# Two places for the squares of q, and modulation products called two loads later

## The chip, the cores and the metric

The kernel runs on one core of one Trainium2 chip. A core has a matrix engine (TensorE, "PE" in the profile), a vector engine (VectorE, "DVE"), an activation engine (ScalarE, "ACT"), a general engine (GpSimd, "POOL") and a synchronisation engine (SyncE, "SP"), which here issues most of the DMA transfers. Each engine works through its own instructions in order and waits on semaphores for the others. The metric is the time of one execution on the device in microseconds. Three runs of the kernel before took 1590.62, 1590.85 and 1592.18 us; the median is 1590.85.

## The reference, cut to what matters

The model is one layer of a diffusion transformer over 1024 latent tokens and 256 context tokens with 1024 channels, all in float32. What the stage of this case computes is:

```python
mod = jax.nn.silu(c) @ w_mod[l] + b_mod[l]                    # six vectors of 1024
mod_c = jax.nn.silu(c_ctx) @ w_mod[l, :, :2 * D_MODEL] + ...  # two vectors of 1024
h = x * (1.0 + scale1) + shift1
h_c = ctx * (1.0 + mods_c[1]) + mods_c[0]
proj = h @ w_in + b_in       # q, k, v of branches A and B, and 2 x 1024 gate logits
q_b = rope(rms_norm(q_b) * q_norm_g)
```

Behind it come windowed attention (branch A) and global attention (branch B), a gated merge, an output projection, a LayerNorm, a SwiGLU feed-forward part with a convolution, and a second LayerNorm. The q norm of branch B needs the mean square of each of the 8 heads of 64 columns for each token.

## The kernel before

Float32 accuracy is had from three passes: each operand is split into a high half (a cast to the fp32r format) and a low half (the rest), and `mm3` (lines 88 to 90) multiplies high by high, low by high and high by low. A split is a cast (line 80 on ACT, 82 on POOL or 84 on VectorE) and a subtraction (line 85) on VectorE or POOL. The names start with "wh" and "wl" for the two halves of a weight.

The projection stage runs in passes. The first makes h from x and projects q of branch B (q1acc). Then a fixed list, `order`, follows: three gate tiles, the pass qa (q of branch A, tokens 0 to 511), four gate tiles, qb (q of branch A, the other tokens), four gate tiles, ka (keys and values of five token tiles), one gate tile, kb, four gate tiles. A gate tile is 2 halves of 24 matmuls; a pass has 8 steps k, each with 3 matmuls for each of its token tiles: 4 in qa and qb, 5 in ka and kb. In each step `prefetch` loads and splits weights some steps ahead, the matmuls follow, then `mods` and `side_step` are called.

Weights are loaded into three "raw" tiles and split into eight "wp" tiles (four pairs of high and low half), so a load waits for the split of an earlier weight, and a cast waits until TensorE is done with an earlier pair. Gate weights have their low half made on POOL, the others on VectorE.

*The ring.* `ht` takes the oldest of 19 free tile places of 128 x 1024 values (`hfree`), and `hput` gives a place back to the end of the list. A tile that is made for a short time is taken and given back at once (`tmp`), so its place comes round again when all free places ahead of it have been used. A load into a place waits until the last use of the tile that had it before. In this stage the ring holds the rope tables, the rows silu(c) and silu(c_ctx) (`sc`, `scc`), the q tiles, the tile of squares `sqq`, and short-lived ones: the modulation rows `wml` (line 648) and the gates `sg` (line 666), which are written to memory (`sgd`).

*Modulation.* Of the 64 products of a column of w_mod with silu(c) or silu(c_ctx), 48 are made in this stage, spread evenly over the matmuls up to the end of ka: `mods` loads a row of 512 KB (line 648) and calls `mod`, one VectorE instruction of 128 x 1024 with a sum (line 186), which shows as CUSTOM_DVE and a short read of the accumulator. The first 16 make `modx`, with which the context tiles `cx` are modulated on ACT (line 631); the others make `modc`.

*The squares.* For each of the 8 token tiles of q of branch B, `qpost` has a step s1: ACT squares the tile into one half of `sqq` (line 280), VectorE sums it by heads (line 283) and scales (284), POOL takes the power -1/2 (285) and makes the negative (320). The step s2 turns q by the rope tables (lines 261 to 269), on VectorE or, for every third tile, on POOL. `sqq` has two halves, used in turn, so the square of tile t overwrites what the reduce of tile t-2 reads.

*The order of instructions.* Nobody writes the order out in this stage. A planner (the tile framework) takes the instructions in the order of the calls as their priority, plays the program through with its own costs, and gives each engine at each moment the first instruction that is ready by its reckoning. The order that comes out is fixed, and on the chip each engine keeps to it, also where an instruction that was ready in the plan has to wait in fact. Only from the first LayerNorm on is the order of TensorE written by hand.

Of the kernel before, what the change touches and what calls it, by code (L numbers as in the profile page):

```python
# [13 lines left out]
P = 128  # L14
# [42 lines left out]
UE = "vector", "vector", "vector", "vector", "vector", "gpsimd", "gpsimd"  # L57
LN2_P = 2, 2, 2
GAP = 1
LN1_S = slice(0, 512), slice(512, 768), slice(768, 1024)  # L60
VOFF = 0.0
VSPAN = 1.0
# [5 lines left out]
def layer_kernel(  # L68
# [25 lines left out]
    def ctile(shape, dt, name):  # L94
        return const.tile(shape, dt, tag=name, name=name)
# [4 lines left out]
    bmc = ctile([P, 48], F32, "bmc")  # L100
# [10 lines left out]
    pqs, nqs = (cvt[:, n * 64:n * 64 + 64].rearrange("p (a b) -> p a b", b=8) for n in (0, 1))  # L111
# [19 lines left out]
    def ht(name, shape=(P, T), dt=F32):  # L131
        hslot[name] = pool, tag = hfree.pop(0)
        return pool.tile(list(shape), dt, tag=tag, name=name, bufs=1)

    def hput(*names):
        for n in names:
            hfree.append(hslot.pop(n))
# [27 lines left out]
    def bias_tile(src, nm):  # L165
        b = ph1.tile([P, 512], F32, tag="bias", name=nm, bufs=2)
        nc.sync.dma_start(b, src.partition_broadcast(P))
        return b
# [11 lines left out]
    def tmp(name):  # L180
        t = ht(name)
        hput(name)
        return t

    def mod(w, row, bias, o):
        nc.vector.tensor_tensor_reduce(out=w, in0=w, in1=row, scale=1.0, scalar=bias, op0=ALU.mult, op1=ALU.add,  # L186
                                       accum_out=o)
# [17 lines left out]
    def modulate(k):  # L205
        wm, x, wr = st1.pop(k)
        w = wsplit(wr, f"qb{k}")
        for j in (0, 1):
            col = j * 8 + k
            mod(wm[j], sc, bmc[:, col:col + 1], modc[:, col:col + 1])  # L210
        hh = hTp.tile([P, T], R32, tag="hT", name=f"hh{k}", bufs=16)
        hl = hTp.tile([P, T], R32, tag="hT", name=f"hl{k}", bufs=16)
        a, b = modc[:, k:k + 1], modc[:, 8 + k:9 + k]
        for s in [slice(0, HALF), slice(HALF, T)] if k == 0 else [slice(0, T)]:
            nc.scalar.activation(hh[:, s], x[:, s], AF.Identity, bias=a, scale=b)
            nc.scalar.activation(x[:, s], x[:, s], AF.Identity, bias=a, scale=b)
            nc.vector.tensor_tensor(out=hl[:, s], in0=x[:, s], in1=hh[:, s].bitcast(F32), op=ALU.subtract)
        hT.append((hh, hl))
        return w
# [7 lines left out]
    w = modulate(0)  # L227
    for k in range(KT):
# [8 lines left out]
        w = wn  # L237
# [20 lines left out]
    def rope(eng, dst, src, H, cs, sn, nm, t1=None, t2=None):  # L258
        if t1 is None:
            t1, t2 = pw(f"rt1{nm}"), pw(f"rt2{nm}")  # L260
        eng.tensor_tensor(out=t1.rearrange("p (h d) -> p h d", d=HD), in0=src.rearrange("p (h d) -> p h d", d=HD),
                          in1=bc(cs, H), op=ALU.mult)
        sv = src.rearrange("p (h r a f) -> p h r a f", r=2, a=2, f=16)
        tv = t2.rearrange("p (h r a f) -> p h r a f", r=2, a=2, f=16)
        sg = sn.rearrange("p (r a f) -> p r a f", r=2, a=2)
        for a in (0, 1):
            eng.tensor_tensor(out=tv[:, :, :, a, :], in0=sv[:, :, :, 1 - a, :],
                              in1=sg[:, :, a, :].unsqueeze(1).to_broadcast([P, H, 2, 16]), op=ALU.mult)
        eng.tensor_tensor(out=dst, in0=t1, in1=t2, op=ALU.add)

    def gfold(dst, gi, t, eng):
        eng.tensor_tensor(out=dst[:, 0], in0=ropec[:, t], in1=gcol[:, gi], op=ALU.mult)
        sv = ropes[:, t].rearrange("p (r a f) -> p r a f", r=2, a=2)
        gv = gcol[:, gi].rearrange("p (r a f) -> p r a f", r=2, a=2)
        dv = dst[:, 1].rearrange("p (r a f) -> p r a f", r=2, a=2)
        for a in (0, 1):
            eng.tensor_tensor(out=dv[:, :, a, :], in0=sv[:, :, a, :], in1=gv[:, :, 1 - a, :], op=ALU.mult)

    def rms_scale(x3, H, nm, sq, ss=None):
        nc.scalar.activation(sq.rearrange("p (h d) -> p h d", d=HD), x3, AF.Square)  # L280
        if ss is None:
            ss = ph1.tile([P, 8], F32, tag="ss", name=f"ss{nm}", bufs=4)[:, 0:H]
        nc.vector.tensor_reduce(out=ss, in_=sq.rearrange("p (h d) -> p h d", d=HD), axis=AX.X, op=ALU.add)
        nc.vector.tensor_scalar(out=ss, in0=ss, scalar1=1.0 / HD, scalar2=QK_EPS, op0=ALU.mult, op1=ALU.add)
        nc.gpsimd.tensor_tensor(out=ss, in0=ss, in1=mhalf[:, 0:H], op=ALU.pow)
        return ss
# [14 lines left out]
    def qtile(br, t):  # L301
        return Q[br, t - t % 2][:, t % 2]

    def qpost(br, t):
        q = qtile(br, t)
        q3 = q.rearrange("p (h d) -> p h d", d=HD)
        if br == 0:
            def r0():
                rope(nc.gpsimd if t % 3 == 2 else nc.vector, q, q, 8, ropec[:, t], ropes[:, t], f"q0_{t}")
            return [r0]  # L310
        st = {}

        def s1():
            st["tb"] = ph1.tile([P, 2, HD], F32, tag="tb", name=f"tbq{t}", bufs=4)
            gfold(st["tb"], 0, t, nc.gpsimd)
            rms_scale(q3, 8, f"q{t}", sqq[0][:, t % 2], pqs[:, t])
            if t == NT - 1:
                sqq.clear()
                hput("sqq")
            nc.gpsimd.tensor_scalar(out=nqs[:, t], in0=pqs[:, t], scalar1=-1.0, scalar2=0.0, op0=ALU.mult, op1=ALU.add)  # L320

        def s2():
            tb = st["tb"]
            rope(nc.gpsimd if t % 3 == 2 else nc.vector, q, q, 8, tb[:, 0], tb[:, 1], f"q1_{t}")
        return [s1] + [lambda: None] * GAP + [s2]

    sqq = [ht("sqq", (P, 2, 512))]
    bias_qb = bias_tile(b_qb, "bias_qb")
    for t in range(NT):
        q_evac(1, t, acc[t], bias_qb)  # L330
# [3 lines left out]
    def kv_alloc():  # L334
        KL.extend(ht(f"KL{h}", dt=R32) for h in range(4))
        KC.append(ht("KC", (P, 4, NC), R32))
        VT.extend(ht(f"VT{t}", (P, 2, 4, P), R32) for t in range(5))
# [3 lines left out]
    def kv_post(t, kv):  # L341
# [28 lines left out]
        def s3():  # L370
# [7 lines left out]
            else:  # L378
                nc.scalar.copy(KC[0][:, :, (t - NT) * P:(t - NT + 1) * P], tr)
        return [s1] + [lambda: None] * GAP + [s2, s3]  # L380

# [254 lines left out]
    late = [(col, scc, modx[:, col:col + 1]) for col in range(16)]  # L636
    late += [(col, sc, modc[:, col:col + 1]) for col in range(16, 48)]

    total = len(late)
    span = [0.0, 0.0]  # L640

    def mods(us):
        span[0] += us
        n = total - len(late)
        for _ in range(min(int(total * span[0] / span[1] + 0.01) - n, len(late))):
            col, row, o = late.pop(0)
            w = tmp(f"wml{len(late)}")
            nc.sync.dma_start(w, wmodT[col])
            mod(w, row, bmc[:, col:col + 1], o)
            if not late:  # L650
                hput("sc", "scc")
                kv_alloc()
# [46 lines left out]
    for n, (gi, k) in enumerate(order):  # L699
# [3 lines left out]
        if gi == "g":  # L703
            for hf in (0, 1):
                last = gate(k, hf)
                mods(3 * KT)
                side_step()
            continue
# [4 lines left out]
        w, c = ready.pop((gi, k))  # L713
# [228 lines left out]
    for f in range(2, KT):  # L942
        bT[1, f] = ht(f"bT1_{f}")
        nc.sync.dma_start(bT[1, f], sgd[KT + f])
        w = wb[f // 2]
# [62 lines left out]
    def drain(keep=0):  # L1008
        while len(pend) > keep:
            pend.pop(0)[1]()  # L1010
            clock[0] = 0.0
# [149 lines left out]
    def y_pair(f, s, first=False):  # L1161
        w = s.stop - s.start
        ps = big(f"y{f}_{s.start}_{w}")
        for a in (0, 1):
            mm_ticked(ps[:, a * HALF:a * HALF + w], wts[f + a], mrg, s)
        for a in (0, 1):
            wout_z(f + a, s, ps[:, a * HALF:a * HALF + w], first and a == 0)

    def ln1(si):
        return ln_steps(zs, zq, LN1_S[si], f"a{si}", emit1, LN1_F[si], *LN1_D[si], order=(0, 4, 1, 5, 2, 6, 3, 7))  # L1170

# [11 lines left out]
    for f in (4, 6):  # L1183
        for si in (1, 2):
            y_pair(f, LN1_S[si])
            if f == 6:
# [68 lines left out]
    def up_start(j, gv):  # L1255
        if (j, gv) not in ups:
            if (j, gv) not in upw:
                up_weights(j, gv)
            ups[j, gv] = big(f"u{gv}_{j}"), upw.pop((j, gv)), set()
        return ups[j, gv]  # L1260
# [37 lines left out]
    for j, gv in ((0, 0), (0, 1), (1, 0)):  # L1298
        up_start(j, gv)
    for si, s in enumerate(LN1_S):  # L1300
        drain((len(LN1_S) - 1 - si) * (KT + 3))
        for j, gv in ((0, 0), (0, 1), (1, 0)):
# [235 lines left out]
    w = s.stop - s.start  # L1538
    nt = w // P

    def pst(n, name):
        return ps4.tile([P, HALF], F32, tag=f"r{n}", name=name)
# [55 lines left out]
    for f, done_ in enumerate(((7,), (0,), (1,), (2, 3))):  # L1598
        o = pst(yb[2 + f % 2], f"yl{f}_{r.start}")[:, 0:w]
# [15 lines left out]
    for t, a in OTO:  # L1615
        o = ot[t, a] = ht(f"ot{t}_{a}", (P, HALF))
        nc.vector.scalar_tensor_tensor(out=o, in0=lnr[0][:, a], scalar=mv[:, t:t + 1], in1=zt[a][t], op0=ALU.mult,
                                       op1=ALU.add)
    for t, a in OTO:
        o = ot[t, a]  # L1620
# [125 lines left out]
```

## Time and profile before

| | |
|---|---|
| median of three runs | 1590.85 us |
| the profiled execution | 1593.3 us |
| its span, first to last instruction | 1591.5 us |
| TensorE busy | 97% of the span |
| VectorE, ACT, POOL busy | 74%, 51%, 46% |
| mean granted TensorE clock | 0.993 |
| projections of this case (first gate to the last step of ka) | about 59 to 261 us |

In the rows of the profile L186 is line 186 of the kernel. An instruction is named by its output and inputs, with tile numbers left out (`wml<-wml,sc,bmc`); "x3" is a number of instructions in a group. In the timeline the columns are the start in us from the begin of the span, the duration, the engine, the line, the operation, the tiles and shapes; brackets hold the idle time of the engine before the instruction and what ended it. In a row of waits there stand the waiting engine and line, whom it waited for, and the sum in us, the number and the longest. In a row of the table by stretches there stand the stretch, its length, then for TensorE, its weight loads, VectorE, ACT and POOL the busy time and the number of instructions, then the granted clock, the DMA share and GB/s. In the view of one tile a row gives the smallest, the median and the largest duration in ns and the first and the last start. "SPq" is the queue in which SP issues DMA transfers.

### The profile page before, as it was taken

To read this page: it belongs to the slowest core of one execution; us is meant where nothing else is said; L and a number is where in the kernel's file an instruction comes from. 1 tells how busy PE (TensorE), PEld (TensorE's weight loads), DVE (VectorE), ACT (ScalarE), POOL (GpSimd) and SP (SyncE) were. 2 spreads that over 40 slices of the span, in tenths; PEclk is the share of its full clock that TensorE was granted. 3 is DMA by queue.
4 is the path that set the end of the run, shared out by engine and by line. 5 is a ranking of instruction groups with operands and counts; after the bars stand their busy time and mean duration, and the time that the engine had idled before them with its cause. 6 is when DMAs were issued, how large, how long until landed. Compare 5 with 4: busy or idle time off the path is not lost.

```text
span 1591.5 us, 22189 instructions
## 1 busy us (share of the span) xinstructions
PE 1537.1 (97%) x7748; PEld 1278.4 (80%) x7748; DVE 1181.3 (74%) x1768; ACT 813.3 (51%) x1450; POOL 730.1 (46%) x727
## 2 busy tenths in 40 slices
PE   6999999999999999999999999999999999999997
PEld 5878788878886887777688888888888888888887
DVE  7797646628888777888674778788888788657884
ACT  5422122448888667688521564454444444535552
POOL 0573212426666556665422453566667665021021
PEclk9999999999999999999999999999999999999999
DMA  9685663322227555532451222333334446996731
GB/s 379 218 309 177 214 204 101 118 79 74 64 81 178 136 127 127 125 84 41 141 173 65 80 80 93 106 106 106 106 106 108 117 116 175 368 274 202 260 107 54
DMA packets 112368, 230.00 MB, mean 145 GB/s; under 512 B 12960, under 2 KB 27808, under 8 KB 112160
## 3 DMA queue, kind: packets, MB, share of 16 engines
q1 hardware_dynamic: 96816, 198.93, 37.9%
q0 software_dynamic: 10400, 20.19, 8.3%
q10 hardware_dynamic: 5040, 9.46, 1.6%
q8 instruction: 61, 1.00, 0.3%
q14 instruction: 51, 0.42, 0.1%
HBM read 177.35 MB, written 65.86 MB: 153 GB/s over the span
## 4 chain that ended last, share of the span: by engine, by line
PE 76%; DVE 8%; DMA 7%; ACT 4%; issue 3%; POOL 2%; SPq 0%; DVEq 0%; ACTq 0%; POOLq 0%
PE ptr L529 4%; PE p L89 3%; PE p L88 3%; PE p L90 3%; PE b L90 3%; PE b L89 3%; PE b L88 3%; PE g L88 2%; PE g L89 2%; PE g L90 2%; PE d L89 2%; PE c L89 2%; PE a L89 2%; PE c L90 2%; PE a L90 2%
## 5 line engine op out<-in xcount | busy, mean ns | idle before, releaser
L539 DVE TENSOR_TENSOR ptl<-ptr,pth 128x512 fp32r<-128x512 f32 x188 | 124.7, 685 | 28.2 <-ACT pth L538 25.8
L529 PE MATMUL ptr<-ident,p 128*128 128x128 f32 x816 | 126.6, 278 | 9.5 <-DVE ptl L539 6.9
L538 ACT CAST pth<-ptr 128x512 fp32r<-128x512 f32 x188 | 106.6, 588 | 56.3 <-PE ptr L529 32.6
L85 DVE TENSOR_TENSOR ld<-rd,hd 128x1024 fp32r<-128x1024 f32 x77 | 94.8, 1249 | 50.8 <-ACT hd L80 48.7
L424 ACT ACTIVATE p<-p,nm 128x1024 f32<-128x1024 f32 (+2 forms) x128 | 125.3, 981 | 11.2 <-DVE p L457 10.5
L529 PEld LDWEIGHTS ptr<-ident,p 128*128 128x128 f32 x816 | 93.7, 140 | 39.8 <-DVE ptl L539 13.5
L80 ACT CAST hd<-rd 128x1024 fp32r<-128x1024 f32 x77 | 79.4, 1049 | 81.9 <-PE p L90 55.5
L550 PE MATMUL av<-pth,VT 128*128 128x512 f32 x236 | 104.6, 443 | 1.0 <-ACT avs L556 0.5
L88 PE MATMUL p<-hd 128*128 128x512 f32 x264 | 103.2, 391 | 0.0
L89 PE MATMUL p<-ld,hd 128*128 128x512 f32 x264 | 102.8, 390 | 0.2 <-DVE ld L85 0.2
L90 PE MATMUL p<-hd,ld 128*128 128x512 f32 x264 | 102.7, 389 | 0.0
L88 PE MATMUL g<-hh,whg 128*128 128x512 f32 x256 | 99.9, 390 | 0.0
L90 PE MATMUL g<-hh,wlg 128*128 128x512 f32 x256 | 99.7, 389 | 0.0
L89 PE MATMUL g<-hl,whg 128*128 128x512 f32 x256 | 99.6, 389 | 0.0
L551 PE MATMUL av<-ptl,VT 128*128 128x512 f32 x236 | 97.6, 414 | 2.0 <-POOL ptl L85 1.9
L85 POOL TENSOR_TENSOR wlg<-wg,whg 128x512 fp32r<-128x512 f32 x32 | 45.5, 1428 | 113.3 <-ACT whg L80 83.1
L457 DVE TENSOR_SCALAR_CACHE_REDUCE p<-s,cvt,nmc 128x1024 f32<-128x1024 f32 x64 | 84.5, 1340 | 12.3 <-PE s L413 11.8
L412 PE MATMUL s<-KL,q 128*128 128x512 f32 (+2 forms) x192 | 76.0, 396 | 2.9 <-ACT p_x L424 2.0
L186 DVE CUSTOM_DVE_ANT_0 wml<-wml,sc,bmc 128x1024 f32<-128x1024 f32 x32 | 44.6, 1406 | 43.0 <-DMA wml<-in_wmodT_dram 40.0
L413 PE MATMUL s<-KL,q 128*128 128x512 f32 (+2 forms) x192 | 71.7, 373 | 0.0
L82 POOL TENSOR_SCALAR pth<-prw 128x512 fp32r<-128x512 f32 x48 | 31.1, 648 | 87.6 <-ACT prw L535 62.1
L80 ACT CAST wS<-s 128x512 fp32r<-128x512 f32 x76 | 45.5, 621 | 45.6 <-POOL s L1077 42.8
(420 smaller groups left out, 4959.4 us busy)
## 6 DMA issues: line engine op xcount, KB each, us to landing
wml<-in_wmodT_dram SPq DMA_DIRECT2D x48, 512.0 KB
ru<-in_w_up_dram SPq DMA_DIRECT2D x38, 512.0 KB
rd<-td SPq DMA_DIRECT2D x55, 256.0 KB
rd<-sd SPq DMA_DIRECT2D x44, 256.0 KB
rd<-in_w_dn_dram SPq DMA_DIRECT2D x33, 256.0 KB
wm<-in_wmodT_dram SPq DMA_DIRECT2D x16, 512.0 KB
wg<-in_w_g_dram SPq DMA_DIRECT2D x32, 256.0 KB
sgd<-sg ACTq DMA_DIRECT2D x32, 256.0 KB
```

Of the source, the lines that this page charges most:

```text
L80: nc.scalar.copy(hi, src)
L85: lo_eng.tensor_tensor(out=lo, in0=src, in1=hi.bitcast(F32), op=ALU.subtract)
L88: nc.tensor.matmul(ps, a[0], b[0], start=start, stop=False, skip_group_check=resumed)
L89: nc.tensor.matmul(ps, a[0], b[1], start=False, stop=False, skip_group_check=resumed)
L90: nc.tensor.matmul(ps, a[1], b[0], start=False, stop=stop, skip_group_check=resumed)
L424: nc.scalar.activation(p, s, AF.Exp, bias=nm[:, h:h + 1], scale=scale, accum_out=sm[:, h:h + 1])
L457: nc.vector.tensor_scalar(out=p, in0=o, scalar1=self.qscale(nqs)[:, hs] if self.br else -1.0, scalar2=self.other[:, hs], op0=ALU.mult, op1 ...
L529: nc.tensor.transpose(tr[:, h * P:(h + 1) * P], self.pslice(h, n), ident)
L538: nc.scalar.copy(hi, tr)
L539: nc.vector.tensor_tensor(out=lo, in0=tr, in1=hi.bitcast(F32), op=ALU.subtract)
L550: nc.tensor.matmul(self.av, v, hi, start=first, stop=False)
L551: nc.tensor.matmul(self.av, v, lo, start=False, stop=self.left == 0)
```

## The change

It has two parts. The squares of q get two tiles of two halves each: tiles 0 and 1 go to the first, 2 and 3 to the second, 4 and 5 to the first again, so a square overwrites what was reduced four tiles earlier. Both tiles are taken where one was taken before, and both are given back in the step s1 of tile 7. The modulation products are called two loads later: `mods` puts a loaded row on a list, and as long as more than two are on it, or no load is left, it calls `mod` for the oldest. The loads are called where they were.

```diff
+MODLAG = 2
...
-            rms_scale(q3, 8, f"q{t}", sqq[0][:, t % 2], pqs[:, t])
+            rms_scale(q3, 8, f"q{t}", sqq[t // 2 % 2][:, t % 2], pqs[:, t])
             if t == NT - 1:
                 sqq.clear()
-                hput("sqq")
+                hput("sqq0", "sqq1")
...
-    sqq = [ht("sqq", (P, 2, 512))]
+    sqq = [ht(f"sqq{n}", (P, 2, 512)) for n in (0, 1)]
...
+    held = []
...
             w = tmp(f"wml{len(late)}")
             nc.sync.dma_start(w, wmodT[col])
-            mod(w, row, bmc[:, col:col + 1], o)
+            held.append((w, row, bmc[:, col:col + 1], o))
+            while held and (len(held) > MODLAG or not late):
+                mod(*held.pop(0))
             if not late:
                 hput("sc", "scc")
                 kv_alloc()
```

## The prediction, made before the changed kernel was run

> **What bounds the kernel now.** The first page of the profile comes first.
>
> ```profile
> span 1591.5 us, 22189 instructions
> PE 76%; DVE 8%; DMA 7%; ACT 4%; issue 3%; POOL 2%; SPq 0%; DVEq 0%; ACTq 0%; POOLq 0%
> ```
>
> Three quarters of the chain that ended last is TensorE work, so another engine counts only where it makes TensorE wait. Both edits sit in the projection stage, so the next view is the TensorE timeline there (start, duration, and in brackets the idle time before an instruction with its releaser).
>
> ```profile
> 91.58 0.39 PE L88 MATMUL accqa<-whqa,hh 128*128 128x512 f32 x1
> 98.97 0.49 PE L88 MATMUL accqa<-whqa,hh 128*128 128x512 f32 x1 [1.79 <-ACT whqa L80]
> 101.36 0.79 PE L89 MATMUL accqa<-wlqa,hh 128*128 128x512 f32 x1 [1.90 <-DVE wlqa L85]
> 120.13 0.39 PE L88 MATMUL g<-hh,whg 128*128 128x512 f32 x1
> 163.65 0.39 PE L88 MATMUL accqb<-whqb,hh 128*128 128x512 f32 x1
> 172.95 0.50 PE L89 MATMUL accqb<-wlqb,hh 128*128 128x512 f32 x1 [0.67 <-DVE wlqb L85]
> 180.81 0.50 PE L89 MATMUL accqb<-wlqb,hh 128*128 128x512 f32 x1 [2.09 <-DVE wlqb L85]
> 182.19 0.63 PE L88 MATMUL accqb<-whqb,hh 128*128 128x512 f32 x1
> 190.51 0.39 PE L88 MATMUL g<-hh,whg 128*128 128x512 f32 x1
> ```
>
> Four gates stand between 120.13 and 163.65: 4 x 2 halves x 24 = 192 matmuls in 43.52 us, so 0.2267 us each with no wait. The pass qa has 8 x 4 x 3 = 96 matmuls, 21.8 us at that rate, and takes 120.13 - 91.58 = 28.6: **6.8 us lost**. qb also has 96 and takes 190.51 - 163.65 = 26.9: **5.1 us lost**. These 11.9 us are all that the change can win on TensorE in these passes. The waits in brackets are 3.7 us of the 6.8 and 2.8 of the 5.1. The rest, 3.1 and 2.3, is matmuls at a lower clock behind the waits (0.63 us for one at 182.19 against 0.39).
>
> Why is qa late? ACT and VectorE in order of time:
>
> ```profile
> 76.12 0.67 DVE L283 TENSOR_REDUCE cvt<-sqq 128x8 f32<-128x512 f32 x1
> ...
> 88.20 0.63 ACT L280 ACTIVATE sqq<-Q 128x512 f32<-128x512 f32 x1 [6.28 <-DVE cvt L283]
> 97.07 0.67 DVE L283 TENSOR_REDUCE cvt<-sqq 128x8 f32<-128x512 f32 x1
> 97.78 0.63 ACT L280 ACTIVATE sqq<-Q 128x512 f32<-128x512 f32 x1 [8.37 <-DVE cvt L283]
> 98.31 1.12 ACT L80 CAST whqa<-wqa 128x512 fp32r<-128x512 f32 x2
> 100.62 0.68 DVE L85 TENSOR_TENSOR wlqa<-wqa,whqa 128x512 fp32r<-128x512 f32 x1
> ```
>
> ACT stood 8.37 us before the square of q tile 7, since its half of sqq was still to be reduced for tile 5 (at 97.07). Queued behind it were the cast of the third qa weight (98.31), behind that its low half (100.62), and then TensorE (101.36). The reduce itself was late because VectorE had waited for modulation loads. The waits of VectorE from 78 to 101, the chain of waits from 155 on, and who waits for whom over the run:
>
> ```profile
> DVE wml L186 <- DMA wml<-in_wmodT_dram: 4.5, 3, 1.9
> ```
> ```profile
> 155.82 4.88 DMA wml<-in_wmodT_dram
> 160.83 1.29 DVE wml L186
> 162.15 3.72 DMA wml<-in_wmodT_dram
> 166.01 1.21 DVE wml L186
> 167.33 3.53 DMA wml<-in_wmodT_dram
> 180.15 0.61 DVE wlqb L85
> ```
> ```profile
> SPq L648 <- DVE modc L186: 40.1, 9, 12.0
> ```
>
> qb is late in another way: a load lands, its product frees a place of the ring, only then does SP issue the next load, and the low halves of the qb weights stand on VectorE between such products.
>
> **The change, part by part.** The tiles concerned:
>
> ```profile
> L648 SPq DMA_DIRECT2D wml<-in_wmodT_dram x48: 327/343/817, 47.5 to 239.7; - x48
> L186 DVE CUSTOM_DVE_ANT_0 wml<-wml,sc,bmc x32: 1269/1285/2312, 104.9 to 243.7; 128x1024 f32<-128x1024 f32 x32
> L186 DVE CUSTOM_DVE_ANT_0 wml<-wml,scc,bmc x16: 1270/1276/2137, 59.7 to 112.9; 128x1024 f32<-128x1024 f32 x16
> DMA wml<-in_wmodT_dram: 44.4, 19
> DVE cvt L283: 22.6, 6
> ```
>
> *Squares.* Nothing is added or removed: eight squares, eight reduces. The square of tile t now needs the reduce of tile t-4, not t-2. Squares 6 and 7 then wait for the reduces of tiles 2 and 3, the last of which started at 76.12, so ACT's 22.6 us of waits (last row; six times) go. The third qa cast then waits for what is next, its own place among the eight wp tiles, which the second half of gate 2 gives back: that half starts 24 x 0.2267 = 5.4 us ahead of 91.58, at 86.1, and has used its first weight pair after 12 matmuls, at 88.9. The low half came 2.3 us behind the cast (100.62 - 98.31), so about 91.2, where TensorE wants it at 97.0 (two steps of 12 matmuls, 2.72 us each, behind 91.58). The cover is 5.8 us, more than the 4.5 us that VectorE waits for loads here; with the cover gone, the stall is what it is now. So the gain is between 0 and 6.8 us, and I take 6.8.
>
> *One ring place fewer* while sqq0 and sqq1 are held. By the code's order the loads have 9 free places instead of 10 until both go back at s1 of tile 7. A load is then issued one release later. Nearest row: 44.4 us in 19 waits, 2.3 us each, on VectorE. In qa that is inside the 5.8 us, so I take 0; without the cover it would be up to 2.3. Places given back in another order change only which old tile a new one overwrites: 0, covered by 14 us or more between the last product (243.7) and the first write of a VT tile:
>
> ```profile
> 259.79 0.41 ACT L348 CAST VT<-kv 128x256 fp32r<-128x256 f32 x1 [1.36 <-DVE kv L727]
> ```
>
> *Products two loads behind.* The same 48 loads on SP and 48 products on VectorE, called later; no DMA is added. But the call is no queue position. The products of scc come first in the code, yet one started at 112.9, after the first of sc at 104.9: the planner dispatches what it holds ready, and the place in the code decides only between instructions that are ready together. Where VectorE is free, as in qb (12.1 us busy in the 20 from 170 to 190, quoted below), a product keeps its place. So for qb the gain lies between 0 and 5.1; I take 0, the nearer row being that of a free engine. Where VectorE is full, products now go behind ropes, reduces and weight splits. That helps the splits, and it holds back what waits for a product: SP, whose 12.0 us wait had the weights of the next gates behind it.
>
> ```profile
> 93.00:126.00 33.00, 29.31 (x117) 23.49 (x116) 33.00 (x49) 7.22 (x12) 21.73 (x16) 0.90 0.80 282
> 170.00:190.00 20.00, 17.25 (x67) 13.36 (x67) 12.10 (x20) 3.72 (x6) 3.16 (x3) 0.91 0.67 225
> 139.15 2.31 DVE L186 CUSTOM_DVE_ANT_0 wml<-wml,sc,bmc 128x1024 f32<-128x1024 f32 x1
> 141.50 0.80 SPq L648 DMA_DIRECT2D wml<-in_wmodT_dram  x2
> 148.01 1.09 ACT L631 ACTIVATE cx<-cx,modx 128x256 f32<-128x256 f32 x2 [12.79 <-DMA cx<-in_ctxT_dram]
> 150.85 3.53 POOL L85 TENSOR_TENSOR wlg<-wg,whg 128x512 fp32r<-128x512 f32 x2 [10.48 <-ACT whg L80]
> 152.77 0.39 PE L88 MATMUL g<-hh,whg 128*128 128x512 f32 x1
> ```
>
> The rows tell one story: VectorE is busy for all 33 us to 126; the product of 139.15 frees a place; SP issues at 141.50; the context tile behind it releases ACT at 148.01; the casts behind that release POOL; and the first low half of gate 6 is done at 150.85 + 3.53 / 2 = 152.6, 0.2 us before TensorE takes it.
>
> *What is late next.* With 6.8 us won in qa, TensorE reaches gate 6 at 146.0. Its weights come earlier only as far as VectorE's full stretch does, by the 4.5 us that it waited for loads, at 148.1. That is a wait of 2.1 us, if SP's order stays; 0 if the planner puts the context loads first. I take 2.1. Whether it costs clock too is open: the 0.67 us wait at 172.95 alone was followed by nothing like the 0.63 of 182.19, and each slow stretch came behind a pair of waits. A single wait is nearer to the first, so clock counts 0, with 2.3 as the other end.
>
> The page "TensorE: Matmul & The Clock Gate" of the Trainium skill (Part 1: The HAM clock gate) says that half rate sets in after an idle window of about 3.4 us. By that rule the new wait costs its own 2.1 us and the sum below is -4.7; with the clock share of qb's pair it is -2.4. The trace does not wholly agree: a wait of 2.09 us was enough at 180.81.
>
> **Sum.** -6.8 + 0 + 0 + 0 + 2.1 = -4.7 us. The profiled execution has 1593.3 us (its span and 1.8 around it), which would be 1588.6; it lies 2.4 above the median of the runs, 1590.85. On the median: **1586.1**. Own range of this case: 1584.0 (nothing given back) to 1588.4 (2.1 + 2.3 given back).
>
> **The rivals.**
> *Both passes are cured.* Speaks for it: qb's low halves stood behind products that waited for loads. Against: VectorE had idle time there, so the planner had no reason to reorder. -6.8 - 5.1 = -11.9: 1579.0.
> *The gain is handed back.* VectorE's full stretch does not move, so gate 6 gets its weights at 152.6 as now: TensorE, there at 146.0, waits 6.6, and 2.3 for the clock: +2.1 net, 1593. With the clock held or the stall coming back within qa: 1590 to 1593. This is also how it looks if the later call changes nothing.
> *Slower: a held-back product keeps SP.* The product of 139.15 comes two loads later. A load comes every (239.7 - 47.5) / 47 = 4.1 us, so at most 8.2 us. SP, context, casts and gate 6 follow; less the 0.2 us of cover and with 2.3 of clock: +10.3 against before, whatever qa won: 1601. Half the delay gives +6.2: 1597. It decides from about 1 us of delay (1 + 2.3 = 3.3). For it: SP already waits 40.1 us for products. Against: after 142 VectorE is seldom full, so a ready product isn't held long.
>
> **How the numbers follow.** A measurement of this kernel tells about 0.2% (3.2 us) from no change: faster below 1587.7, slower above 1594.0. The forecast gets 0.41, both cured 0.17, handed back 0.16, slower 0.26. Of the forecast about 0.02 ends above 1587.7; so faster is 0.56, same 0.18, slower 0.26. The range runs from 1578.5, just below both cured, to 1599, which leaves out the top of the slower case, some 0.1, and a little below.
>
> **What would show it.** Right: no wait of ACT for the reduces at the squares; qa within 22 to 24 us; scc products later than 112.9. A gate 6 that waits for its low half is the part given back; a qb still 5 us long shows that the later call moved nothing there. Wrong: SP waits longer than 12.0 us for a product, with gate weights behind; or the planner's new order puts a stall into attention, which no row of before can show.

## The result and the profile after

The changed kernel takes **1597.35 us** (median of 6 runs, 1593.21 to 1598.54) against 1590.85 (6 runs of the kernel before beside it, 1590.16 to 1592.56): a ratio of **1.0036, 95% interval 1.0023 to 1.0048**. It is slower by 6.5 us on the medians; the whole interval lies above the 0.2% that the prediction counted as telling. The forecast was 1586.1. (One execution among the runs below, of e13, took 6130 us where its others took 1588 to 1595; it is left out of that kernel's figures.)

The first page of the changed kernel, its span and the engines' shares of the chain that ended last:

```profile
span 1591.3 us, 22199 instructions
PE 81%; DVE 8%; ACT 4%; issue 3%; DMA 3%; POOL 1%; SPq 0%; DVEq 0%; ACTq 0%; POOLq 0%
```

This span is 0.2 us shorter than the one of before, although the kernel is slower. The execution that was profiled is the fastest of the six (1593.21 us), and the one of before (1593.3) was among that kernel's slowest. So spans are compared by stages here, and both kernels were profiled once more (e8 and e9 below). TensorE's timeline after, at the starts of the passes and where it waited longest:

```profile
91.41 0.39 PE L89 MATMUL accqa<-whqa,hh 128*128 128x512 f32 x1
98.68 0.50 PE L90 MATMUL accqa<-wlqa,hh 128*128 128x512 f32 x1 [1.44 <-DVE wlqa L86]
115.94 0.39 PE L89 MATMUL g<-hh,whg 128*128 128x512 f32 x1
160.03 0.39 PE L89 MATMUL accqb<-whqb,hh 128*128 128x512 f32 x1
162.07 0.50 PE L90 MATMUL accqb<-wlqb,hh 128*128 128x512 f32 x1 [1.66 <-DVE wlqb L86]
175.12 0.79 PE L90 MATMUL accqb<-wlqb,hh 128*128 128x512 f32 x1 [7.29 <-DVE wlqb L86]
192.70 0.39 PE L89 MATMUL g<-hh,whg 128*128 128x512 f32 x1
```

qa takes 115.94 - 91.41 = 24.5 us (28.6 before), the four gates 44.1 (43.5), and **qb 192.70 - 160.03 = 32.7 us (26.9)**. One wait of 7.29 us stands in qb where the longest was 2.09. In qa, ACT and VectorE did this:

```profile
88.70 0.62 ACT L81 CAST whqa<-wqa 128x512 fp32r<-128x512 f32 x1 [1.85 <-PE g L90]
92.07 1.27 DVE L187 CUSTOM_DVE_ANT_0 wml<-wml,scc,bmc 128x1024 f32<-128x1024 f32 x1
93.27 1.28 DVE L187 CUSTOM_DVE_ANT_0 wml<-wml,scc,bmc 128x1024 f32<-128x1024 f32 x1
96.20 1.29 DVE L187 CUSTOM_DVE_ANT_0 wml<-wml,scc,bmc 128x1024 f32<-128x1024 f32 x1 [1.04 <-DMA wml<-in_wmodT_dram]
97.42 1.20 DVE L86 TENSOR_TENSOR wlqa<-wqa,whqa 128x512 fp32r<-128x512 f32 x1
```

The third cast comes at 88.70, released by TensorE and no longer behind a square. Its low half comes only at 97.42: three products (rows above, one waiting for its load), a rotation and two reduces stand between. In qb the same happens on a larger scale (ACT, VectorE and SP's queue in order of time):

```profile
157.98 0.62 ACT L81 CAST whqb<-wqb 128x512 fp32r<-128x512 f32 x1 [0.47 <-ACT sg L670]
161.33 1.29 DVE L86 TENSOR_TENSOR wlqb<-wqb,whqb 128x512 fp32r<-128x512 f32 x2
163.42 8.84 SPq L650 DMA_DIRECT2D wml<-in_wmodT_dram  x4
165.47 1.28 DVE L187 CUSTOM_DVE_ANT_0 wml<-wml,sc,bmc 128x1024 f32<-128x1024 f32 x1 [2.85 <-DMA wml<-in_wmodT_dram]
168.18 1.28 DVE L187 CUSTOM_DVE_ANT_0 wml<-wml,sc,bmc 128x1024 f32<-128x1024 f32 x1 [1.42 <-DMA wml<-in_wmodT_dram]
173.16 1.28 DVE L187 CUSTOM_DVE_ANT_0 wml<-wml,sc,bmc 128x1024 f32<-128x1024 f32 x1 [1.73 <-DMA wml<-in_wmodT_dram]
174.37 1.29 DVE L86 TENSOR_TENSOR wlqb<-wqb,whqb 128x512 fp32r<-128x512 f32 x2
175.09 0.93 SPq L627 DMA_DIRECT2D wqb<-in_w_qa_dram  x2
178.31 1.37 ACT L81 CAST whqb<-wqb 128x512 fp32r<-128x512 f32 x2 [8.89 <-DMA wqb<-in_w_qa_dram]
```

The third weight of qb was cast at 157.98, and its low half came 16.4 us later, at 174.37: four products stand between, and VectorE waits ahead of three of them for their rows. Two of the four rows are among those that SP issued one by one over 8.84 us, each into a place that an earlier product has to free. The low half frees the raw tile, so the next weight loads go out at 175.09 and ACT's cast waits 8.89 us for them. The very first low half of qb is late already: in the views of the tile wlqb it comes at 154.1 before and at 161.3 after, behind seven products. SP was given the loads of six of them ahead of the second qb weight, and that of the seventh behind the third.

The order that the planner gave VectorE and SP in qb differs between the two programs. Numbers are modulation rows, counted down (on VectorE the product, on SP the load); brackets are the weights of qb (on VectorE the low half, on SP the load); r is a rotation of q of branch A, g6_1 the second half of gate 6's weights.

```
VectorE before  19 r 17 14 29 23 [qb0] [qb1] 22 16 20 [qb2] 11 [qb3] 15 [qb4]
VectorE after   30 24 28 17 21 27 19 [qb0] [qb1] 14 22 20 16 [qb2] [qb3] 15 18 [qb4]
SP before       g6_1 cx2 cx3 [qb0] 23 [qb1] [qb2] 22 [qb3] [qb4] 16 20 11 15 [qb5]
SP after        30 g6_1 [qb0] 24 28 17 21 27 [qb1] [qb2] 19 14 [qb3] 22 [qb4] 20 16 15 18 [qb5]
```

### The profile page after: what moved, and what is told of

Its sections match the earlier page's. It is cut to its first block, busy times and chain, and to the rows that moved or that the text cites. A ratio compares the mean times of both kernels' runs of the same rounds, so it can differ in the third digit from the quotient of the medians.

```text
span 1591.3 us, 22199 instructions
## 1 busy us (share of the span) xinstructions
PE 1533.0 (96%) x7748; PEld 1274.8 (80%) x7748; DVE 1177.1 (74%) x1768; ACT 813.1 (51%) x1450; POOL 736.4 (46%) x727
## 4 chain that ended last, share of the span: by engine, by line
PE 81%; DVE 8%; ACT 4%; issue 3%; DMA 3%; POOL 1%; SPq 0%; DVEq 0%; ACTq 0%; POOLq 0%
PE ptr L530 5%; PE p L91 4%; PE p L90 4%; PE p L89 4%; PE b L91 3%; PE b L90 3%; PE b L89 3%; PE g L89 3%; PE g L90 3%; PE g L91 3%; PE s L413 2%; PE av L551 2%; PE av L552 2%; PE d L89 2%; PE c L89 2%
## 5 line engine op out<-in xcount | busy, mean ns | idle before, releaser
L86 POOL TENSOR_TENSOR wlg<-wg,whg 128x512 fp32r<-128x512 f32 x32 | 50.3, 1580 | 122.6 <-ACT whg L81 75.5
```

Source lines behind the costliest of these rows:

```text
L86: lo_eng.tensor_tensor(out=lo, in0=src, in1=hi.bitcast(F32), op=ALU.subtract)
```

## The experiments

Every profiled execution can be read by one figure. From the first gate to the gate behind qb there are three gates, qa, four gates and qb, which take 119.7 us with no wait (32.64 + 21.76 + 43.52 + 21.76). "Lost" is what a kernel takes beyond that. The times are us; "median" and ratio are of all runs, the other columns of one execution.

| kernel | qa | four gates | qb | lost | span | span - lost | median | ratio to before, 95% interval |
|---|---|---|---|---|---|---|---|---|
| before | 28.6 | 43.5 | 26.9 | 11.9 | 1591.5 | 1579.6 | 1590.85 | |
| e9: before again | 25.4 | 43.9 | 25.5 | 7.8 | 1586.6 | 1578.8 | | |
| after | 24.5 | 44.1 | 32.7 | 14.3 | 1591.3 | 1577.0 | 1597.35 | 1.0036 (1.0023 to 1.0048) |
| e8: after again | 28.3 | 43.5 | 33.6 | 18.4 | 1596.0 | 1577.6 | | |
| e1: squares alone | 27.2 | 43.5 | 32.8 | 16.5 | 1594.0 | 1577.5 | 1597.10 | 1.0041 (1.0028 to 1.0054) |
| e2: lag alone | 28.2 | 43.5 | 25.1 | 9.8 | 1590.0 | 1580.2 | 1593.63 | 1.0016 (1.0006 to 1.0027) |
| e3: held place alone | 26.7 | 43.9 | 33.2 | 16.8 | 1597.2 | 1580.4 | 1599.51 | 1.0053 (1.0040 to 1.0067) |
| e4: after, place back early | 28.8 | 43.5 | 24.2 | 9.4 | 1588.8 | 1579.4 | 1591.10 | 1.0005 (0.9994 to 1.0017) |
| e5: after, qb's low halves on POOL | 28.8 | 43.5 | 29.4 | 14.6 | 1593.9 | 1579.3 | 1593.09 | 1.0015 (1.0006 to 1.0025) |
| e6: before, products behind low halves | 30.0 | 43.5 | 21.8 | 8.2 | 1588.4 | 1580.2 | 1590.23 | 0.9994 (0.9985 to 1.0004) |
| e7: e4, products behind low halves | 29.1 | 43.5 | 21.8 | 7.3 | 1584.7 | 1577.4 | 1588.30 | 0.9986 (0.9976 to 0.9996) |
| e10: after, products behind low halves | 29.4 | 43.5 | 21.8 | 7.7 | 1588.4 | 1580.7 | 1588.52 | 0.9986 (0.9977 to 0.9996) |
| e11: e7, rotations on VectorE | 21.8 | 43.5 | 21.8 | 0.0 | 1579.6 | 1579.6 | 1580.90 | 0.9940 (0.9926 to 0.9954) |
| e12: e6, rotations on VectorE | 21.8 | 43.5 | 21.8 | 0.0 | 1579.5 | 1579.5 | 1581.26 | 0.9941 (0.9928 to 0.9955) |
| e13: before, rotations on VectorE | 23.0 | 46.2 | 29.2 | 11.3 | 1589.7 | 1578.4 | 1592.47 | 1.0012 (1.0003 to 1.0020) |
| e14: after, rotations on VectorE | 21.8 | 43.7 | 38.4 | 16.8 | 1595.2 | 1578.4 | 1597.91 | 1.0048 (1.0036 to 1.0060) |

Span less lost lies between 1577.0 and 1580.7 in all sixteen, while lost goes from 0 to 18.4: where two executions differ by more than 3.7 us, they differ in this stretch.

**Which part does it: e1, e2, e3.** One part of the change each. e1 is the changed kernel with products called at their loads:

```diff
-MODLAG = 2
+MODLAG = 0
```

> The two tiles of squares with the second ring place that they take, products called right behind their loads (lag 0). Theory A (the second ring place does the harm in qb, since the loads of modulation rows behind it come in another order; the later call does little): qb takes about 32.7 us as in the changed kernel, qa about 24.5, and the time is that of the changed kernel, 1595 to 1599. Theory B (the later call does the harm in qb): qb takes 26.9 as before, qa 24.5, and the time is 1586 to 1588.

e2 is the other half: the changed kernel with one tile of squares, as before, and the lag of two loads (shown against the kernel before, cut).

```diff
-    sqq = [ht("sqq", (P, 2, 512))]
+    sqq = [ht("sqq0", (P, 2, 512))]
...
-            mod(w, row, bmc[:, col:col + 1], o)
+            held.append((w, row, bmc[:, col:col + 1], o))
+            while held and (len(held) > MODLAG or not late):
+                mod(*held.pop(0))
```

> One tile of squares as before, products called two loads behind. Theory A: qb 26.9 us as before; qa between 24.5 and 28.6, since ACT still waits for the reduces; time 1587 to 1591. Theory B: qb 32.7, qa 28.6, time 1596 to 1600.

e3 is the kernel before with a ring place that nothing uses, held as long as the second tile of squares is:

```diff
+    hslot["idle"] = hfree.pop(0)
...
-                hput("sqq")
+                hput("sqq", "idle")
```

> One tile of squares and lag 0 as before, but a second ring place is taken with it and given back with it, and nothing is ever written there. Theory A: qb about 32.7 us, qa not cured (28 or more), time 1597 to 1601, worse than the changed kernel. Theory B: like before, 1590 to 1592.

e3 has neither the second tile's use nor the lag, and it is the slowest of the three (1599.51), with the changed kernel's qb (33.2 us). VectorE's timeline of e3 has the same four products between the second and the third low half; the first and the last of these, the low halves behind them, and TensorE's wait:

```profile
166.62 1.28 DVE L186 CUSTOM_DVE_ANT_0 wml<-wml,sc,bmc 128x1024 f32<-128x1024 f32 x1 [2.54 <-DMA wml<-in_wmodT_dram]
...
174.74 1.28 DVE L186 CUSTOM_DVE_ANT_0 wml<-wml,sc,bmc 128x1024 f32<-128x1024 f32 x1 [1.76 <-DMA wml<-in_wmodT_dram]
...
175.94 1.28 DVE L85 TENSOR_TENSOR wlqb<-wqb,whqb 128x512 fp32r<-128x512 f32 x2
176.68 0.80 PE L89 MATMUL accqb<-wlqb,hh 128*128 128x512 f32 x1 [7.41 <-DVE wlqb L85]
```

So the held place alone gives the slow qb. In the programs of e1 and e3 the order in qb, of VectorE and of SP, is that of the changed kernel. The lag alone costs 0.16%, a little more than was expected (1593.63 us against 1587 to 1591), with a qb of 25.1 us and no wait over 1.41 us in it; in the presence of the second place it makes no difference that shows (1597.10 without, 1597.35 with).

**The place given back early: e4.** The changed kernel, with the first tile of squares given back behind tile 5, its last use, and the second behind tile 7:

```diff
+            if t == NT - 3:
+                hput("sqq0")
             if t == NT - 1:
                 sqq.clear()
-                hput("sqq0", "sqq1")
+                hput("sqq1")
```

> The changed kernel, but the first tile of squares gives its ring place back at the step s1 of tile 5, its last user, and not at that of tile 7. Theory A: the loads fall back into their old order, qb 26.9 us, qa 24.5, time 1586 to 1588, faster than both kernels. Theory B: like the changed kernel, 1595 to 1599.

qb is back at 24.2 us and the time at before's (1591.10): two tiles' longer hold is the whole harm, and the order in qb is again that of the kernel before, row for row. The gain that was expected beyond that did not come, since qa stays at 28.8 us. There too the cast was early (89.63) and the low half late (100.25), behind products.

**Where the low halves stand: e5, e6.** e5 makes qb's low halves of the changed kernel on POOL, which no product uses:

```diff
-        ready[gi, k] = wsplit(wr, f"{nm}{k}"), c
+        ready[gi, k] = wsplit(wr, f"{nm}{k}", "gpsimd" if gi == 3 else "vector"), c
```

> The changed kernel, but the low halves of the qb weights are made on POOL, which is idle in qb, and no longer on VectorE. Theory A (they stood on VectorE behind products that wait for their loads): qb goes from 32.7 us to 22 to 24, the time to 1586 to 1589. Theory C (the weight loads stand behind the loads of modulation rows on SP, so it does not matter which engine splits): qb stays above 28 us, the time above 1592.

1593.09 us and a qb of 29.4, which is what theory C allowed; but qb does fall, by 3 to 4 us from 32.7 or 33.6. So theory A has a part in it too. SP's queue and ACT show what was left:

```profile
165.87 9.11 SPq L650 DMA_DIRECT2D wml<-in_wmodT_dram  x3
175.07 0.38 SPq L627 DMA_DIRECT2D wqb<-in_w_qa_dram  x1
180.07 0.62 ACT L81 CAST whqb<-wqb 128x512 fp32r<-128x512 f32 x1 [7.90 <-DMA wqb<-in_w_qa_dram]
```

Three row loads, each waiting for a place, hold SP for 9.11 us with the weight load behind them. The order harms through both queues, VectorE's and SP's.

e6 leaves the kernel before as it is, but for one thing: each product is put behind the last low half that VectorE has been given, so that the planner can't draw it forward (cut: `lowq[0]` holds that low half).

```diff
-            mod(w, row, bmc[:, col:col + 1], o)
+            with tc.issue_after(lowq[0]):
+                mod(w, row, bmc[:, col:col + 1], o)
```

> The kernel before (one tile of squares, lag 0) with one thing added: each product is queued on VectorE behind the low half of a weight that was called before it, so the planner can no longer put products ahead of splits. Theory A: qa 22 to 25 us and qb 22 to 23, no waits of TensorE for low halves of 2 us or more, time 1580 to 1584. If products late in the queue instead keep SP from its loads (my rival in the prediction), gates or qb show new waits and the time is 1591 or more.

qb has no wait left (21.8 us), but the time is the same as before (0.9994): qa became the longest of all, 30.0 us. What qb won was given back there, and both the qa and the time that were expected were missed.

**Both together: e7, e10.** e7 is e4 with the edit of e6; e10 is the changed kernel itself, its two places held to tile 7, with that edit.

> The kernel of e4 (two tiles of squares, the first place given back at tile 5, lag 2) with the same order of products behind splits. Theory A: as e6 or up to 3 us faster, since ACT does not wait for reduces: qa 22 to 24, qb 22 to 23, 1578 to 1583.

> The changed kernel (two ring places held to the last tile, products two loads behind) with one thing added: each modulation product is issued behind the last low half that VectorE has. Theory A (the held place does its harm only by the order that the planner gives VectorE, low halves of qb behind products): qb falls from 32.7 to 22 to 25 us, and the time to 1587 to 1591. Theory D (the held place also starves SyncE, whose weight loads of qb stand behind product loads that wait for a place): qb stays over 27 us and the time over 1593.

They come out alike (1588.30 and 1588.52), and e10 is 8.8 us faster than the changed kernel with the very same use of the ring. In its program the order in qb is

```
VectorE   30 [qb0] [qb1] 28 27 26 [qb2] [qb3] 25 [qb4] 24 [qb5] [qb6] 23 [qb7]
SP        30 g6_1 cx2 cx3 [qb0] 24 28 27 [qb1] [qb2] 22 [qb3] [qb4] 21 20 19 18 [qb5] [qb6] [qb7]
```

and SP's row loads still wait for places (the first row below), but the weight loads have left before the time they are needed (the last two rows; the view of the tile wlqb has no waiter on TensorE any more):

```profile
158.98 5.91 SPq L654 DMA_DIRECT2D wml<-in_wmodT_dram  x4
164.98 4.10 SPq L631 DMA_DIRECT2D wqb<-in_w_qa_dram  x3
186.45 0.39 PE L89 MATMUL g<-hh,whg 128*128 128x512 f32 x1
```

So the held place costs nothing by itself (e10 against e7: 0.2 us); it costs by the order that the planner makes of it. That the place starves SP whatever the order is thereby refuted. (The edit moves SP's order too, by way of the planner: which of the two queues matters more is not separated by it; e5 puts 3 to 4 of the 11 to 12 us that qb loses on VectorE's.) The expectation for e7 (qa cured as well) was missed: qa stays at 29.1. VectorE's and POOL's timeline of e7 say why:

```profile
90.68 1.29 POOL L274 TENSOR_TENSOR Q<-rt1q,rt2q 128x512 f32<-128x512 f32 x1
92.00 0.76 DVE L272 TENSOR_TENSOR rt2q<-Q,tbq 128x256 f32<-128x256 f32 x2 [6.33 <-POOL Q L274]
92.68 0.68 DVE L86 TENSOR_TENSOR wlqa<-wqa,whqa 128x512 fp32r<-128x512 f32 x1
```

VectorE stands 6.33 us before a rotation, since POOL's own rotation has not yet released the temporary rt2q that both use, and a low half of qa is queued behind. TensorE waits 1.51 us for that one, and 3.49 us at 102.74 for the next but one, ahead of which VectorE has three products and the rest of two rotations to finish.

**What is left in qa: e11, e12.** e11 is e7 with the second rotation of tiles 2 and 5 taken from POOL to VectorE; e12 is e6 with the same, that is, the kernel before with both additions and nothing of the change.

```diff
-            rope(nc.gpsimd if t % 3 == 2 else nc.vector, q, q, 8, tb[:, 0], tb[:, 1], f"q1_{t}")
+            rope(nc.vector, q, q, 8, tb[:, 0], tb[:, 1], f"q1_{t}")
```

> As e7 (place given back at tile 5, products behind low halves), and the second rotation of tiles 2 and 5, now on GpSimd, is done on VectorE. In e7 VectorE sat idle for 6.33 us up to 92.00 waiting for GpSimd's rotation to free the rotation's temporaries, with the low half of qa behind it. Theory E (that wait is what is left of qa's loss): qa falls from 29.1 to 22 to 25 us and the time to 1582 to 1585. Against it: about 4 us more work on VectorE only moves the low halves back; qa stays at 27 to 29 us and the time at 1587 to 1590.

> The kernel before (one place of squares, products at their loads) with the two additions of e11: products behind low halves, all second rotations on VectorE. It leaves out just the change itself, its squares and its lag, and so tells what the second place of squares is worth where the order is no longer in the way. If ScalarE's waits for the reduces were what kept qa's casts late (the prediction's step on the squares), qa stays at 25 to 28 us and the time at 1584 to 1588. If the order of VectorE's queue was the whole loss, qa and qb come out at 21.8 us as in e11 and the time at 1580 to 1582.

Both have no wait in qa and qb at all, and are the fastest kernels here: 1580.90 and 1581.26 us, 0.6% faster than before. TensorE's timeline of e12, and from the view of its tile of squares what ACT waited for there (us in all, times):

```profile
90.87 0.39 PE L88 MATMUL accqa<-whqa,hh 128*128 128x512 f32 x1
112.63 0.39 PE L88 MATMUL g<-hh,whg 128*128 128x512 f32 x1
156.15 0.39 PE L88 MATMUL accqb<-whqb,hh 128*128 128x512 f32 x1
177.91 0.39 PE L88 MATMUL g<-hh,whg 128*128 128x512 f32 x1
```
```profile
  DVE cvt L287: 10.3, 6
```

In e12 a square still needs the reduce two tiles back, and ACT waits six times for one, 10.3 us in all where it was 22.6; qa is 21.76 us long all the same. The wait before the square of tile 7 is 1.42 us where it was 8.37, and that square runs at 82.98, not at 97.78 (ACT's timeline of e12):

```profile
82.98 0.64 ACT L284 ACTIVATE sqq<-Q 128x512 f32<-128x512 f32 x1 [1.42 <-DVE cvt L287]
```

So ACT's long stall goes without a second place of squares, once VectorE's queue is in order: it was a result of that queue. The second place of squares and the lag (e11) add nothing that shows.

**Rotations alone: e13, e14.** The last edit by itself, on the kernel before and on the changed one.

> The kernel before with the one edit that e11 and e12 have beyond e7 and e6: the second rotation of tiles 2 and 5 on VectorE, not on GpSimd. Theory E1 (qa's loss is VectorE standing idle for GpSimd's rotation, with or without an order for the products): qa falls from 25 to 29 us to 22 to 24, qb stays at 25 to 27, and the time is 1584 to 1587. Theory E2 (both are needed: without the order, products that wait for their loads still stand ahead of qa's low halves): qa stays at 26 us or more and the time within 0.2% of before, 1588 to 1593.

> The changed kernel with the same single edit. Under E1, qa falls to 22 to 24 us; qb, whose order the held ring place sets, stays at 32 to 34 us; so the time is 1591 to 1595 against 1597.35 without the edit. Under E2, qa stays at 26 us or more, and the time at 1595 to 1599.

qa is cured in both (23.0 and 21.8, one profile each, outside the 24.5 to 28.6 of the four profiles without the edit), so it is moving the rotations that cures qa. But nothing is won: in e13 the four gates take 2.7 us more, with a wait for a gate's low half, and qb 29.2; in e14 qb grows to 38.4 us. There VectorE still has its products ahead of the low halves, and TensorE, there earlier, waits longer; that is read from the traces and not isolated by a run. The times that E1 gave (1584 to 1587 for e13, 1591 to 1595 for e14) were missed: its qa was right, its qb was not. The table by stretches of e14 (columns as in the prediction's; the granted clock is the third figure from the end) shows what qb's two waits, 5.06 and 5.52 us, do to the clock: 0.81 there, 1.00 around the cured qa.

```profile
90.00:120.00 30.00, 30.00 (x134) 24.63 (x133) 29.31 (x51) 7.07 (x12) 18.05 (x12) 1.00 0.73 252
160.00:196.00 36.00, 27.68 (x97) 22.00 (x98) 20.79 (x34) 5.86 (x10) 4.27 (x3) 0.81 0.70 240
```

Which of three things cures qa when the rotations move (POOL's own time, the shared temporaries, or the new order that the planner makes of them) was not separated. A wait of VectorE for POOL's rotation shows in qa only where the products stand behind low halves (7.05 us in e6, 6.33 in e7 and e10), and not in the profiles of the kernel before or of the changed one.

**The same program again: e8, e9.**

> The changed kernel once more, to see how far a pass differs from one execution to the next: qb within 1 us of 32.7 if the order of instructions sets it; qa between 24 and 28, since the squares-only kernel with nearly the same order had 27.2.

> The kernel before, unchanged, for a second profile beside the one that the prediction used (span 1591.5 us, passes qa 28.55 and qb 26.86 us). If the passes are the same from execution to execution, both come out within 0.5 us of that. If they are not, then qa between 25 and 29, qb between 23 and 27, and a span of 1588 to 1592.

TensorE's longest waits in e8, the second profile of the changed kernel:

```profile
101.10 0.80 PE L90 MATMUL accqa<-wlqa,hh 128*128 128x512 f32 x1 [4.70 <-DVE wlqa L86]
176.95 0.79 PE L90 MATMUL accqb<-wlqb,hh 128*128 128x512 f32 x1 [7.58 <-DVE wlqb L86]
```

qa is 28.3 us in this execution and 24.5 in the first; the kernel before has 28.6 and 25.4. So the 4 us that the first profile seemed to show as won in qa lie within what one program does from one execution to the next. qb doesn't vary like that: 26.9 and 25.5 before, 32.7 and 33.6 after.

## Why the prediction was wrong, step by step

The means of the two profiles of each kernel give the balance: qa 27.0 before and 26.4 after, -0.6; the four gates 43.7 and 43.8, +0.1; qb 26.2 and 33.1, **+7.0**. Sum +6.5, and the medians differ by 6.5. That the two agree so closely is luck: qa alone varies by 3 us and more, and the spans of the same four profiles differ by 4.6 us in the mean.

*Squares, -6.8.* The mechanism came in the main as told, the result didn't. ACT's waits for the reduces fell from 22.6 us in six waits to 7.7 in three (below), and the third cast came at 88.70, where 88.9 was forecast.

```profile
ACT sqq L281 <- DVE cvt L284: 7.7, 3, 4.0
```

The term that failed is "the low half came 2.3 us behind the cast": it was 8.7 us (88.70 to 97.42) in the first profile, and over 10 in e4. The 2.3 had been read where ACT itself came late, so VectorE had worked off its queue in the meantime. The cover of 5.8 us was set against VectorE's 4.5 us of waits for loads, not against the products that also stood in the queue. So freeing ACT did not shorten qa: with the cast early, the mean of qa is 0.6 us less than before, and e4 has 28.8. That ACT's stall was a result of VectorE's late reduces, not a cause of its own, is what e12 shows: with VectorE's queue in order the long stall is gone with one tile of squares.

*One ring place fewer, 0, at most 2.3.* **This is the step that failed and turned the sign.** It was priced as a load that goes out one release later, with every queue's order kept. Measured alone (e3) it costs 8.5 us (1599.51 against 1590.98, 0.40% to 0.67%). With the place missing, the planner reckons other loads and products ready at other times and lays out another order for VectorE and SP, with four products, not three, between the second and the third low half of qb, and with five row loads, not one, between its first two weight loads. e10 has the place missing and the order mended, and is 8.8 us faster: the order is the price. The sentence that places given back in another order "change only which old tile a new one overwrites" failed with it. Whether the missing place or the other order of giving back moves the planner was not separated; in the order of the calls 10 places are free in qb in both kernels. (The count was off by one too, and nothing hung on it: up to the end of qa 10 places are free where it was 11, then 8 where it was 9.)

*Products two loads behind, 0 in qb.* The reading that a call is no queue position holds: the order of products and weights in qb with the lag alone is the same as without it, and e1 and the changed kernel are equal. The sign that was named for it, products with scc later than 112.9 us, did not come: the last starts at 105.9. Alone, e2 costs 2.65 us on the medians (1593.63 against 1590.98), of which its profile shows no place. But the bounds of qb, "between 0 and 5.1", left out a loss, and they were argued from the lag alone. What the other edit might do in qb, over 60 us behind the last square, was not asked.

*What is late next, +2.1 at gate 6.* Gate 6 doesn't wait in either profile of the changed kernel. In the first TensorE reached it at 149.15, ahead of the 152.6 at which its first low half was done before; so here a wait was to be expected, had SP's order stayed. It did not stay: the new order has the context loads ahead of the weights of gates 3 and 5, where two of them stood ahead of gate 6's, and POOL is done with that half by 139.9 (its timeline after; the last of the three):

```profile
135.29 4.61 POOL L86 TENSOR_TENSOR wlg<-wg,whg 128x512 fp32r<-128x512 f32 x3
```

That is the case for which the prediction gave 0, "if the planner puts the context loads first". That a gain is handed back elsewhere is real: where qa is cured and the products stay where they are, the gain is handed back, in e13 at a gate by a wait of 2.37 us and in qb, in e14 all of it in qb.

*The rivals.* The one on the slower side gave 1597 at half the delay, near the measured time, but that is luck. Its cause was the later call, and e1 is as slow without it; and the place was another: SP's longest wait for a product is 6.4 us where 12.0 was the mark, and no gate's weights stood behind it, but those of qb.

```profile
SPq L650 <- DVE modc L187: 42.4, 13, 6.4
```

"Both passes cured", 1579.0, was against the change's nature but right as a price: e11 and e12 cure both and measure 1580.90 and 1581.26.

*The clock, 0 or 2.3.* A single short wait costs no clock here up to 2.37 us (e13's gate). In TensorE's timelines of e4 (first two rows), e2 (next two) and e3 (last two), the wait and a matmul behind it:

```profile
180.72 0.50 PE L90 MATMUL accqb<-wlqb,hh 128*128 128x512 f32 x1 [2.03 <-DVE wlqb L86]
181.29 0.39 PE L89 MATMUL accqb<-whqb,hh 128*128 128x512 f32 x1
```
```profile
100.67 0.80 PE L90 MATMUL accqa<-wlqa,hh 128*128 128x512 f32 x1 [3.75 <-DVE wlqa L86]
101.27 0.63 PE L91 MATMUL accqa<-whqa,hl 128*128 128x512 f32 x1
```
```profile
99.88 0.80 PE L89 MATMUL accqa<-wlqa,hh 128*128 128x512 f32 x1 [2.80 <-DVE wlqa L85]
100.48 0.63 PE L90 MATMUL accqa<-whqa,hl 128*128 128x512 f32 x1
```

Behind 2.03 us the matmuls keep 0.39 us, and e4's qb loses 0.4 us beyond the wait; behind 3.75 they take 0.63, and e2's qa loses 2.65 beyond it (28.16 - 21.76 - 3.75); behind 2.80 in e3 they take 0.63 too. The page "TensorE: Matmul & The Clock Gate" of the Trainium skill (Part 1: The HAM clock gate) puts the idle window at about 3.4 us. The waits of 2.03 and 3.75 us agree with it; the single wait of 2.80 us and the pair of 0.67 and 2.09 us in the kernel before, with slow matmuls behind them, do not. Nor is a pair a rule: in e13 waits of 0.66 and 2.37 us, 8.3 us apart, have none behind them. What beyond the length of the wait decides stays open.

## What to carry to other kernels

Where a planner fixes each engine's order, a tile place more or less is not priced by the wait for that place: it can change the order of every queue that loads through the ring, also far behind the edit, so the range must take in what a worse order would cost at the next tight stage. A wait that is inferred from one chain (ACT behind a reduce) shows what came last there; how long the next engine's queue is must be read for that engine by itself, with what stands between the cast and its low half. And where a small instruction that TensorE needs shares a queue with work that waits for other engines and for DMAs, every such wait ahead of it has to go: on the kernel before, the order of the products alone (e6, 0.9994) and the rotations alone (e13, 1.0012) won nothing, and both together won 0.6%. With the order set, the held place made no difference (e7 and e10), and with both set neither did the squares and the lag (e11 and e12).

## What the runs showed that was not expected

One and the same program gives 25.4 or 28.6 us for qa (before), 24.5 or 28.3 (after): 3 to 4 us from run to run in a single stage, all of it waits for a half of a weight and the clock behind them. One profile of each kernel would have told a gain in qa that isn't there.

Curing one pass can lengthen the next by as much as was won: in e14 qa is 3 to 7 us shorter than in the changed kernel's profiles, and qb 5 to 6 us longer, with two waits of 10.6 us together and 6.0 us of slower clock (38.4 - 21.8 - 10.6).
